# An HBM-to-HBM half shift on one core: two DMA queues of 256-row copies become one queue of 512-row copies with an uneven start

## The chip, the core and the metric

The kernel runs on one core of a Trainium2 chip. It uses no compute engine for the data: everything is done by DMAs from one tensor in HBM to another, carried out by the core's 16 DMA engines. The DMAs are issued by two instruction sequencers, SP (SyncE, `nc.sync`) and ACT (ScalarE, `nc.scalar`); each of them feeds its own queue, which the profile calls q1 (SP) and q10 (ACT), and both queues run on the same 16 DMA engines. The metric is the device time in microseconds (us).

## The reference

```
x: 8192 x 8192, float32
out = np.fft.ifftshift(x)
```

Both sides are even, so this is a shift by half in both directions: `out[r, c] = x[(r + 4096) % 8192, (c + 4096) % 8192]`. The four quadrants of the matrix change places diagonally. No number is changed. A row is 32 KB (32,768 bytes), half a row 16 KB (16,384 bytes); the matrix is 268.44 MB, which is read once and written once, as 16,384 half rows.

## The kernel before

The work is cut into blocks of 256 rows (`ENGINES * per` = 16 x 16). For each of the 32 blocks, two DMAs are issued, one on each queue: one copies the left halves of the 256 output rows (from the right halves of the source rows), the other the right halves (from the left ones). In even blocks SP has the left halves and ACT the right ones, in odd blocks it is the other way round. So each queue gets 32 DMAs of 256 half rows, 4 MB each.

The access pattern of a DMA, `[[C, 16], [16 * C, 16], [1, 4096]]`, has 16 as its outermost size, and this is what spreads it over the 16 DMA engines: engine e gets rows e, e + 16, e + 32 and so on of the block, 16 half rows of 16 KB each, and each half row is one packet. At any time the engines thus work on neighbouring rows, and an engine's next packet of the same queue lies 16 rows (512 KB) further on. An engine that has work in both queues takes packets from the two in turn.

The Tile framework gives the DMAs eight semaphores in rotation, four for each queue here. From the fifth DMA of a queue on, the sequencer waits before the issue until the DMA four earlier on that queue has landed. Hence at most four DMAs of a queue are in flight.

Of the kernel before, what the change touches and what calls it, by code (L numbers as in the profile page):

```python
# [1 line left out]

# [4 lines left out]


ENGINES = 16


@with_exitstack
def kernel(
    ctx: ExitStack,
    tc: tile.TileContext,
    x: bass.AP,
    out: bass.AP,
):
    nc = tc.nc
    R, C = x.shape  # L20
    hr = R // 2
    hc = C // 2
    per = 16
    rows = ENGINES * per

    def copy(queue, row, h, step):

        dims = [[C, ENGINES], [step * C, per], [1, hc]]
        queue.dma_start(
            out=bass.AP(out.tensor, out.offset + row * C + h, dims),  # L30
            in_=bass.AP(x.tensor, x.offset + (row + hr) % R * C + hc - h, dims),
        )


    for n, row in enumerate(range(0, R, rows)):
        left = n % 2 == 0
        copy(nc.sync, row, 0 if left else hc, ENGINES)
        copy(nc.scalar, row, hc if left else 0, ENGINES)


# [1 line left out]
_INS = ['x']  # L42
_OUTS = [((8192, 8192), 'float32')]


def kernel(**inputs):
    import numpy as _np
    import concourse.bacc as _bacc
    import concourse.tile as _tile
    from concourse import mybir as _mybir  # L50
    from concourse.bass_utils import run_bass_kernel_spmd as _run

    nc = _bacc.Bacc("TRN2", target_bir_lowering=False, num_devices=1)  # L53
    arrays, args = {}, []
    for name in _INS:
        a = _np.ascontiguousarray(inputs[name])
        if a.dtype.kind in "iu":
            a = a.astype(_np.int64)
        arrays[f"in_{name}_dram"] = a
        args.append(nc.dram_tensor(f"in_{name}_dram", a.shape, _mybir.dt.from_np(a.dtype), kind="ExternalInput").ap())  # L60
    for i, (shape, dtype) in enumerate(_OUTS):
        dt = _mybir.dt.from_np(_np.dtype(dtype))
        args.append(nc.dram_tensor(f"out_{i}_dram", shape, dt, kind="ExternalOutput").ap())
    with _tile.TileContext(nc) as tc:
        kernel(tc, *args)
    r = _run(nc, [arrays], core_ids=[0])
    got = tuple(r.results[0][f"out_{i}_dram"] for i in range(len(_OUTS)))
    return got[0]
```

## Time and profile before

| What | Value |
|---|---|
| Time of three runs | 813.11, 813.71, 814.12 us; median 813.71 us |
| Span of the profiled execution | 813.2 us |
| Bytes read, bytes written | 268.44 MB each, 660 GB/s together over the span |
| DMA packets | 17,408: 16,384 of 16 KB and 1,024 semaphore writes |
| DMA issues | 32 on SP, 32 on ACT, 4096 KB each, about 101 us from issue to landing |
| Work of compute engines | 0.2 us (four small memsets of GpSimd) |

The profile's span runs from the first to the last instruction; the time lies 0.5 us above it in the median. A row of the DMA part names the queue, its packets, the megabytes and the time that its packets took, as a share of the span of all 16 DMA engines. Packets come in two sizes only, so from such a row the mean time of one 16 KB packet can be worked out: share x stretch x 16, divided by the number of packets. The trace also holds start, duration, size and queue of each packet, without the number of the engine.

### The profile page before, as it was taken

What the parts mean: (1) busy time and instruction counts of PE and PEld (TensorE: products, weight loads), DVE (VectorE), ACT (ScalarE), POOL (GpSimd) and SP (SyncE); (2) the same over time, 40 slices, a digit from 0 to 9 for tenths busy, and PEclk for the clock granted to TensorE, in tenths of its full rate; (3) what the DMA queues carried; (4) which work ended last, traced back from release to release, by engine and by line L of the source; (5) the groups of instructions that cost most, each with busy time, mean ns of one, the idle gap of its engine ahead of it and who ended that gap; (6) DMA issues with size and microseconds to landing.
All of it is one profiled execution on the core that took longest, in us unless ns stands there. A gap on an engine that the chain in (4) does not pass through costs nothing. (4 is left out here: it accounts for less than half of the span.)

```text
span 813.2 us, 109 instructions
## 1 busy us (share of the span) xinstructions
POOL 0.2 (0%) x4
## 2 busy tenths in 40 slices
POOL 0000000000000000000000000000000000000000
DMA  9999999999999999999999999999999999999998
GB/s 303 336 326 331 334 329 323 330 338 333 330 333 330 334 334 330 335 334 330 325 338 330 336 330 334 334 333 331 341 331 330 334 334 330 333 328 336 331 334 276
DMA packets 17408, 268.44 MB, mean 330 GB/s; under 512 B 1024, under 2 KB 1024, under 8 KB 1024
## 3 DMA queue, kind: packets, MB, share of 16 engines
q1 hardware_dynamic: 8704, 134.22, 50.4%
q10 hardware_dynamic: 8704, 134.22, 48.6%
HBM read 268.44 MB, written 268.44 MB: 660 GB/s over the span
## 5 line engine op out<-in xcount | busy, mean ns | idle before, releaser
L53 POOL MEMSET const-bfloat16-1.0<- 128x1 bf16 x1 | 0.1, 102 | 0.0
L53 POOL MEMSET const-uint8-127<- 128x1 uint8 x1 | 0.1, 101 | 0.0
L53 POOL MEMSET const-float32-0.0<- 128x1 f32 x1 | 0.1, 99 | 0.2 <-issue 0.2
L53 POOL MEMSET const-float32-1.0<- 128x1 f32 x1 | 0.1, 98 | 0.0
## 6 DMA issues: line engine op xcount, KB each, us to landing
out_dram<-in_x_dram SPq DMA_DIRECT2D x32, 4096.0 KB, 101.2
out_dram<-in_x_dram ACTq DMA_DIRECT2D x32, 4096.0 KB, 101.1
```

The lines of the kernel that those rows point to most:

```text
L53: nc = _bacc.Bacc("TRN2", target_bir_lowering=False, num_devices=1)
```

## The change

All DMAs go on SP's queue; ACT issues none. The left halves of all 8,192 rows are copied first (from row 0 to the end), and then all right halves. A DMA covers 512 half rows, 32 packets an engine (one of them 464, because the left pass of the first 4,096 rows is 48 rows short of eight whole ones).

The first 48 left half rows go in five DMAs of 14, 12, 10, 8 and 4 rows. Their outermost size is that number and not 16, so they lie on the first 14, 12, 10, 8 and 4 engines with one packet each: engines 0 to 3 get five packets, 4 to 7 four, 8 and 9 three, 10 and 11 two, 12 and 13 one, 14 and 15 none. Then the ordinary DMAs begin at row 48, with the same number of packets for every engine (1,021). Altogether there are 37 DMAs instead of 64, on eight semaphores in rotation, so up to eight are in flight, and the ninth and later ones wait for the one eight earlier.

```diff
-    per = 16
-    rows = ENGINES * per
-    def copy(queue, row, h, step):
-        dims = [[C, ENGINES], [step * C, per], [1, hc]]
+    def copy(queue, row, col, dims):
         queue.dma_start(
-            out=bass.AP(out.tensor, out.offset + row * C + h, dims),
-            in_=bass.AP(x.tensor, x.offset + (row + hr) % R * C + hc - h, dims),
+            out=bass.AP(out.tensor, out.offset + row * C + col, dims),
+            in_=bass.AP(x.tensor, x.offset + (row + hr) % R * C + (col + hc) % C, dims),
         )
-    for n, row in enumerate(range(0, R, rows)):
-        left = n % 2 == 0
-        copy(nc.sync, row, 0 if left else hc, ENGINES)
-        copy(nc.scalar, row, hc if left else 0, ENGINES)
+    unlike = (14, 12, 10, 8, 4)
+    steps = 32
+
+    def walk(queue, row, end, col):
+        while row < end:
+            n = min(steps, (end - row) // ENGINES)
+            copy(queue, row, col, [[C, ENGINES], [ENGINES * C, n], [1, hc]])
+            row += ENGINES * n
+
+    row = 0
+    for n in unlike:
+        copy(nc.sync, row, 0, [[C, n], [1, hc]])
+        row += n
+    walk(nc.sync, row, hr, 0)
+    walk(nc.sync, hr, R, 0)
+    walk(nc.sync, 0, R, hc)
```

## The prediction

> **What bounds the kernel now.** I read the page from the top: the span, the slices, the queues, the issues.
>
> ```profile
> span 813.2 us, 109 instructions
> ...
> DMA  9999999999999999999999999999999999999998
> GB/s 303 336 326 331 334 329 323 330 338 333 330 333 330 334 334 330 335 334 330 325 338 330 336 330 334 334 333 331 341 331 330 334 334 330 333 328 336 331 334 276
> DMA packets 17408, 268.44 MB, mean 330 GB/s; under 512 B 1024, under 2 KB 1024, under 8 KB 1024
> ## 3 DMA queue, kind: packets, MB, share of 16 engines
> q1 hardware_dynamic: 8704, 134.22, 50.4%
> q10 hardware_dynamic: 8704, 134.22, 48.6%
> HBM read 268.44 MB, written 268.44 MB: 660 GB/s over the span
> ...
> out_dram<-in_x_dram SPq DMA_DIRECT2D x32, 4096.0 KB, 101.2
> out_dram<-in_x_dram ACTq DMA_DIRECT2D x32, 4096.0 KB, 101.1
> ```
>
> The DMA engines are busy in every slice, at an even rate. A DMA lands 101 us after its issue, four times the 25 us that 32 packets of an engine take (16 of each queue), so the engines always have work waiting and issue bounds nothing after the start. What counts is the time of one 16 KB packet: each engine has 1,024 of them. For q1 it is 0.504 x 813.2 x 16 / 8,192 = 800 ns, for q10 772 ns, the mean 786. In the packet records a third of them take 608 to 615 ns, and hardly any less: this is what an engine takes when nothing is in its way. The other 170 ns of the mean are contention, and 1,024 x 786 ns = 805 us of the span is packets. The rest is 2.2 us before the first packet and some 6 us of end (the last packets of the engines end between 809.2 and 812.0 us), semaphore writes and gaps.
>
> So the question is what the changed pattern does to these 786 ns: one queue, so that at any time all engines write left halves and read right ones (later the reverse), whereas now half the packets in flight do the one and half the other. Two stretches show one queue alone. First, the start; the DMA rows of the stretch from 3 to 5 us, then from 4.9 to 5.5 us and from 5.5 to 6.3 us:
>
> ```profile
> q1 hardware_dynamic: 48, 0.79, 97.9%
> ...
> q10 hardware_dynamic: 15, 0.25, 104.1%
> ...
> q1 hardware_dynamic: 15, 0.25, 101.7%
> ```
>
> While only q1 was there, a packet took 0.979 x 2 x 16 / 48 = 653 ns. Then q10 joined with 666 ns, and the next round of q1 took 868. Second, the end: from 807.3 us on q10 is alone, and 49 packets took 0.390 x 5.9 x 16 / 49 = 751 ns (the semaphore writes are nothing in it).
>
> ```profile
> q10 hardware_dynamic: 65, 0.80, 39.0%
> ```
>
> The rate by stretches (us, length, POOL, clock, DMA share, GB/s written):
>
> ```profile
> 3.10:5.10 2.00, 0.00 (x0) 1.00 1.04 426
> 5.10:7.00 1.90, 0.00 (x0) 1.00 0.91 310
> 9.00:12.00 3.00, 0.00 (x0) 1.00 0.98 328
> 20.00:40.00 20.00, 0.00 (x0) 1.00 0.98 331
> 400.00:420.00 20.00, 0.00 (x0) 1.00 1.01 337
> ```
>
> The 426 GB/s hold for 2 us; 10 us after the start the rate is already that of the whole run.
>
> **The change, part by part.** *The start.* The issues of SP on the time line (start, length, count; four in 2.77 us, so one in 0.69):
>
> ```profile
> 0.73 2.77 SPq L29 DMA_DIRECT2D out_dram<-in_x_dram  x4
> ```
>
> Five small DMAs in front put the first ordinary one's issue at 0.73 + 5 x 0.69 = 4.2 us, and with the 1.44 us that now lie between the first issue and the first packet (2.17 us) its packets begin at 5.6 us. Engines 0 to 3 are then through with their five: 2.17 + 0.97 (first round) + 4 x 0.65 = 5.75 us. Engines 14 and 15 have nothing until 5.6 us. So the issue pitch equals a packet's time, and all engines enter row 48 within about 0.2 us of each other: the five packets of lead are waited off, not kept. If a DMA of 14 rows issues in, say, two thirds of the time (bound: the records show no small one), the spread is about 1.3 us, less than the 2 to 3 us between the first and the last engine that the semaphore landings of one DMA show now anyway. Cost: engines 14 and 15 have 1,021 packets to do at 5.6 us, where they now have about 1,019.2 left (3.4 us at 653 ns, the first 965); engines 0 to 3 have 1,026 instead of 1,024. Both ways about +1.4 us. Between 0 (small issues that are quick) and 2.6 us (engines 14 and 15 idle 3.4 us, only 1 us of it made up).
>
> *Number of DMAs.* 37 instead of 64: 27 semaphore packets of 9 ns fewer for each engine, -0.25 us. Longer DMAs change nothing else: with eight in flight, 256 packets an engine wait instead of 128. The new waits of SP (the ninth DMA for the first, and so on) have only SP's later DMAs behind them and about 200 us of queued work as cover; the ninth's own is over at about 4 us, and three long DMAs (96 packets, 75 us) are queued by then.
>
> *ACT's issues* go; they cost nothing now (cover: the same queued work).
>
> *One queue, one half at a time.* Three readings of a packet:
> - q1's mean, 800 ns. q1 runs ahead: its DMAs land 4.6 us before q10's of the same block, so it is the first to touch a 32 KB row, and q10 follows in the other half. That the follower is 28 ns cheaper can be a gain from the row just visited. With one pass for each half, every packet is a first visit: 14 ns x 1,024 = +14.7 us.
> - Windows of 0.3 us in the records, sorted by how many of the 16 engines are on q1: 335 GB/s at 8 to 10, 320 to 322 at 0 to 4, 331 at 12 to 16, mean 332. The nearer to one queue, the slower: 0.3% to 3.7%, +2 to +30 us. Single packets say so more sharply: a q1 packet that starts with 2 others on q1 takes 753 ns, with 14 others 872.
> - The stretches alone: 653 ns (-136 us) at the start, 751 (-36 us) at the end. The start is three rounds out of an idle memory and its rate is gone 2 us later; at the end engines are already dropping out, which helps those that remain.
>
> I take the first, which lies inside the second and rests on 16,384 packets instead of 97: +14.7. Sum: +1.4 - 0.25 + 14.7 = +15.8 us on the profiled 813.2, 829.0; with the 0.5 us by which the median is above the span, 829.5. Ends: 751 ns gives 813.7 - 36 + 1 = 779, and 320 GB/s gives 813.7 + 30 + 1 = 845.
>
> The Trainium skill (HBM Reference, Specifications) gives about 716 GB/s for a stack; by it an estimate of the packets' least time is 536.9 MB / 716 = 750 us in place of 805, if both tensors share one stack, and the 653 ns of the start, 804 GB/s both ways, could only be a short-lived loan from buffers. No row of this trace shows where the tensors lie.
>
> **The rivals.**
> 1. *Faster: the two halves disturb each other.* With two queues, reads of one fall among writes of the other in the same halves; alone, they are apart. For it: both stretches alone, and the jump from 653 to 868 ns one round after q10 came. Against it: the sorted windows. Price: the end's 751 ns, 779 us; it decides if a packet in mid-run takes less than 785 ns. The start's 653 ns held for all gives 679 us; I give that little.
> 2. *Faster: the lead is kept*, and engines that stand in other row groups collide less. For it: the records' rate swings with a period of 6.3 us, four packets of each queue (64 rows), between 321 and 340 GB/s, so where the rows lie matters. Levelled at the best mixture, 335 GB/s, this is 1% less: 807 us. Against it: the issue arithmetic above, by which the change does not do what it says.
> 3. *No change.* The same 16 engines carry the same bytes at 786 ns: 813.7 + 1.4 - 0.25 = 814.9 us. The flat slices (323 to 341) speak for a limit that no order moves; the 28 ns between the queues against. The Trainium skill says this too (DMA: Bandwidth & Descriptors, Issuing engines are not separate DMA queues): several issuing engines save only issue time; by that rule alone it would be 814.9 us.
>
> **How the numbers follow.** Slower by first visits and by like traffic: 0.51, its own range 818 to 848, with a few in a hundred beyond. Rival 1: 0.30, between 700 and 805. Rival 2: 0.09, 800 to 811. No change: 0.10, of which the start's cost puts 0.04 above the bound. This kernel's measurement can tell about 0.2% (1.6 us) from no change. So faster 0.39, same 0.06, slower 0.55. The likeliest is 829.5. The range leaves out a tenth at each side: 770 to 848.
>
> **What would show it.** The first visits: the queue row of the changed kernel, one queue at a mean of about 800 ns a packet and slices of 322 to 328 GB/s, in both halves of the run; slices of 345 and more are rival 1, and 332 is rival 3. The start: first long packets of all engines at 5.5 to 6 us. The lead: landings of one DMA spread over 2 to 3 us, as now, and not over 4. Issues: 37 on SP, 8,192 KB in the median, about 200 us to landing. The prediction is wrong above all if the cheaper q10 has another cause than the row just visited, such as an order among queues that one queue doesn't have.

## The result: 0.5% slower

| | kernel before | changed kernel |
|---|---|---|
| Median of six runs | 813.63 us | 818.10 us |
| Ratio of the two, 95% interval | | 1.0051 (1.0034 to 1.0068) |
| The same on a second chip, 23 and 12 runs | 810.57 us | 814.53 us |
| Ratio there | | 1.0040 (1.0019 to 1.0061) |
| Span of the profiled execution | 813.2 us | 816.2 us |

The change costs 4.5 us. I had forecast 15.8, so the direction was right and the size more than three times too large. The page of the changed kernel, slices, queue and issues:

```profile
span 816.2 us, 82 instructions
...
DMA  8999999999999999999999999999999999999998
GB/s 275 331 333 327 338 328 334 332 334 336 340 331 332 331 332 328 329 337 332 333 328 328 333 327 330 327 337 331 333 332 334 334 333 331 326 335 328 333 330 272
DMA packets 16944, 268.44 MB, mean 329 GB/s; under 512 B 560, under 2 KB 560, under 8 KB 560
## 3 DMA queue, kind: packets, MB, share of 16 engines
q1 hardware_dynamic: 16944, 268.44, 98.9%
HBM read 268.44 MB, written 268.44 MB: 658 GB/s over the span
...
out_dram<-in_x_dram SPq DMA_DIRECT2D x31, 8192.0 KB, 106.9
```

One queue now carries everything at 0.989 x 816.2 x 16 / 16,384 = 788 ns a packet: neither the 800 of the old q1 nor the 751 of the lone queue at the old end, but the old mean of both queues, 786. The slices after the first are those of before. The first is lower, 275 against 303 GB/s.

So I split the span in its first 10 us, its last 10 us and what lies between. The stretches of the kernel before, then of the changed one (start and end, length, POOL, clock, DMA share, GB/s written):

```profile
0.00:10.00 10.00, 0.20 (x4) 1.00 0.79 280
803.20:813.18 9.98, 0.00 (x0) 1.00 0.64 215
```

```profile
0.00:10.00 10.00, 0.20 (x4) 1.00 0.61 211
806.20:816.17 9.97, 0.00 (x0) 1.00 0.60 204
```

In the first 10 us the changed kernel moves 2.11 MB instead of 2.80. At the later 332 GB/s the missing 0.69 MB are 2.1 us. In the last 10 us it lacks 0.11 MB, 0.3 us. What is left for the middle is 263.5 MB in 793.2 us before (332.2 GB/s) and 264.3 MB in 796.2 us after (332.0 GB/s): 0.6 us. Of the 3.0 us between the spans, the start has two thirds.

The medians differ by 1.5 us more than these two spans. In every other profiled run of this case the time is 1.7 to 1.8 us above the span, so the profiled execution of the kernel before took about 815 us, some 1.3 us more than its median. Of the 4.5 us between the medians, the start and the end thus have about 2.4; the other 2 us (0.25%) lie somewhere in the run, and these two profiles don't show where.

How the start loses them is on SP's time line (start, length, instructions): the first small DMA, the first long one, and then the eighth and ninth together.

```profile
0.73 0.97 SPq L26 DMA_DIRECT2D out_dram<-in_x_dram  x1
...
4.74 0.64 SPq L26 DMA_DIRECT2D out_dram<-in_x_dram  x1
...
6.08 22.25 SPq L26 DMA_DIRECT2D out_dram<-in_x_dram  x2
```

A DMA of 14 rows doesn't issue faster than one of 256: the five take 0.97, 0.80, 0.74, 0.66 and 0.60 us, and the first long one follows at 4.74 us. In the packet records only 4.4 of 16 engines are busy between 5.5 and 6.0 us, and all of them only from 8.5 us on; before, all were busy from 2.5 us. Weighed by engines, the start stands still 2.0 us longer.

### The profile page after: what moved, and what is told of

It is laid out like the page before. It is cut to its first block, busy times and chain, and to the rows that moved or that the text cites. A ratio compares the mean times of both kernels' runs of the same rounds, so it can differ in the third digit from the quotient of the medians.

```text
span 816.2 us, 82 instructions
## 1 busy us (share of the span) xinstructions
POOL 0.2 (0%) x4
## 6 DMA issues: line engine op xcount, KB each, us to landing
out_dram<-in_x_dram SPq DMA_DIRECT2D x31, 8192.0 KB, 106.9
```

## The experiments

The changed kernel itself was among them:

> The changed kernel again, beside the others on one chip. On a chip where the kernel before takes 822 us, 0.4% to 0.6% above it; if the costs add, one queue without the uneven start (0.28%) and its start and end (about 1.1 us, 0.14%) make 0.42%.

Measured: 1.0040 (1.0019 to 1.0061), as in the table above. In its first 10 us it moved 193 GB/s, where `e5_two_halves` (below), without the uneven start, moved 275 on the same chip. At 332 GB/s the missing 0.82 MB are 2.5 us.

The chips differ: the kernel before takes 811 to 823 us on them. Each ratio is taken on one chip, against runs of the kernel before there.

### Undoing the uneven start

`e1_plain` is the changed kernel with

```diff
-    unlike = (14, 12, 10, 8, 4)
+    unlike = ()
```

> The changed kernel without the uneven start: one queue, 512 rows a DMA, left halves then right ones. If the uneven start alone costs the time (idle engines at the start, a wider end) and one queue is free: 814 to 815 us, mean packet 786 to 788 ns, landings of a DMA spread over 2 to 3 us. If one queue with one half at a time costs the 2 ns a packet that the changed kernel shows, and the start nothing: 816 to 818 us. If the uneven start has hidden what I forecast for one queue, so that engines in step suffer: packets of 800 ns and 825 to 830 us.

Measured: 1.0028 (1.0008 to 1.0048), and 797 ns a packet on a chip where the kernel before takes 822.5 us:

```profile
span 824.4 us, 77 instructions
...
q1 hardware_dynamic: 16896, 268.44, 99.1%
...
0.00:10.00 10.00, 0.20 (x4) 1.00 0.82 280
```

The last line is its first 10 us: without the five small DMAs it moves 280 GB/s there, as the kernel before does, and not 211. So the loss at the start belongs to the uneven start.

> One queue, 512 rows a DMA, left halves then right ones, no uneven start, again. If the single queue costs something of its own: 0.1% or more above two queues with the same order of halves, which run beside it. If the order of halves is all there is: both 0.15% to 0.3% above the kernel before.

The second time, on another chip, it was 1.0019 (0.9999 to 1.0039). So one queue without the uneven start is about 0.2% slower than the kernel before, hardly more than can be told from nothing, and the rival that in-step engines suffer is out in the size expected (825 to 830 us where the kernel before takes 814). Something smaller of the kind isn't excluded: in the two profiles of this kernel the rate from 20 to 200 us is 321 and 326 GB/s, and 329 to 331 later, a rise that the two profiles of the changed kernel don't have (331 to 333 throughout). With the uneven start the ratio is 1.0051 and 1.0040, some 0.2% higher, which fits the 2.0 us of the start; the differences are near their intervals' width, so the first 10 us of the profiles are the stronger evidence for it.

### The first visit to a row

`e3_far` takes away the second visit, on which I had put the forecast:

```diff
-        copy(nc.scalar, row, hc if left else 0, ENGINES)
+        copy(nc.scalar, (row + hr) % R, hc if left else 0, ENGINES)
```

> The kernel before, but ACT copies the half rows of a block 4,096 rows away from SP's, so that no engine's queue comes back to a 32 KB row that the other has just visited. If the second visit to a row is what makes q10 28 ns cheaper than q1 (the step of the prediction): both queues near 800 ns and 825 to 829 us. If the difference belongs to the queues or their order: q1 again near 800, q10 near 772, and 812 to 815 us.

Measured: 1.0004 (0.9985 to 1.0023). The queues:

```profile
span 821.2 us, 109 instructions
...
q1 hardware_dynamic: 8704, 134.22, 49.8%
q10 hardware_dynamic: 8704, 134.22, 49.4%
```

That is 798 and 792 ns. The expected 825 to 829 us were 1.4% to 1.9% above the 814 us of the kernel before, and nothing of this came. That both queues are near 800 ns is no sign of it: the chip is slower, the kernel before takes 822.5 us there, and by this its mean packet would be 786 x 822.5 / 813.7 = 794 ns (an estimate, it has no profile on that chip). The mean of `e3_far` is 795.

Nor does the gap between the queues come from the second visit alone. `e5_two_halves` (below) copies all left halves before the right ones, so no queue comes back to a row that the other has just visited, and still one queue is cheaper:

```profile
span 810.8 us, 109 instructions
...
q1 hardware_dynamic: 8704, 134.22, 50.2%
q10 hardware_dynamic: 8704, 134.22, 49.0%
```

These are 795 and 776 ns, and 797 and 791 in its second profile. The gap differs between two profiles of one program, and with every packet a first visit the measured ratios are 1.0001 to 1.0017. The step is refuted: 800 ns wasn't the price of a first visit. What sets the gap stays open.

### What the total is: fewer engines, and reads alone

If the total is fixed, engines that take less than their part must run undisturbed. `e4_twelve` copies with 12 engines, the kernels below with 13 and 14 (the edit is on the kernel before; `...` stands for lines left out):

```diff
-    for n, row in enumerate(range(0, R, rows)):
...
+    def walk(queue, row, end, col):
+        while row < end:
+            n = min(32, (end - row) // 12)
+            if n:
+                dims = [[C, 12], [12 * C, n], [1, hc]] if n > 1 else [[C, 12], [1, hc]]
+                size = 12 * n
+            else:
+                size = end - row
+                dims = [[C, size], [1, hc]]
...
+            row += size
+
+    walk(nc.sync, 0, hr, 0)
+    walk(nc.sync, hr, R, 0)
+    walk(nc.sync, 0, hr, hc)
+    walk(nc.sync, hr, R, hc)
```

> One queue, left halves then right ones, no uneven start, but only 12 of the 16 DMA engines, 1,364 packets each. If a limit on all traffic together (332 GB/s each way) sets the packet's 786 ns: twelve engines at the undisturbed 611 ns would move 322 GB/s, below the limit, so packets of 611 to 640 ns and 845 to 885 us. If each engine is held up by every other one it meets: 611 + 175 x 11/15 = 739 ns and about 1,015 us.

```profile
span 838.4 us, 93 instructions
...
GB/s 277 323 312 314 321 326 322 326 322 323 324 323 324 323 323 324 323 325 322 324 324 324 324 324 324 324 323 323 325 322 325 322 325 322 325 322 325 323 325 255
...
q1 hardware_dynamic: 16928, 268.44, 74.9%
```

840.2 us for one run, a little under the expected 845 to 885, beside 822.5 of the kernel before on that chip. The packets take 0.749 x 838.4 x 16 / 16,384 = 613 ns, in the records 99% of them at the undisturbed 611. A quarter of the engines is gone, the time is 2% longer, and the contention has vanished.

> As with twelve engines, but 13 engines, 1,260 packets each. Undisturbed they would move 349 GB/s each way, above what 16 engines get. If all traffic together has a fixed limit near 330 GB/s: packets near 640 ns and 815 to 828 us, as 16 engines. If it is the crowding of 16 engines that lowers the limit: packets of 611 to 625 ns and 780 to 800 us, 3% to 5% under the kernel before.

> 14 engines, 1,170 packets each; undisturbed 376 GB/s each way. Fixed limit: packets near 690 ns and 815 to 828 us. Crowding: packets between those of 13 and 16 engines, and 790 to 815 us.

Measured: 1.0236 (1.0203 to 1.0268) and 1.0362 (1.0329 to 1.0395), slower than either expectation. The slices of the 13 engines:

```profile
GB/s 281 330 330 335 331 337 335 333 331 336 331 332 333 330 334 333 335 335 333 331 336 331 331 336 334 334 331 334 319 329 333 332 325 329 331 336 329 323 217 176
...
q1 hardware_dynamic: 17028, 268.44, 79.3%
```

The mean packets, 642 and 681 ns, are as a fixed limit would have them. Through most of the run 13 engines move 332 GB/s, as 16 do, and 14 engines 328 in this stretch from 20 to 780 us:

```profile
20.00:780.00 760.00, 0.00 (x0) 1.00 0.85 328
```

The limit is there: undisturbed they would have moved 349 and 376. The times are longer because the engines don't share it alike. In the landings of the second DMA of 13 engines, 5 engines are done at 43.2 to 43.5 us and 8 at 46.1 to 47.1; the 5 go on at 19.5 us a DMA at first, undisturbed (32 x 611 ns), and the 8 fall ever further behind. At the end these are alone: from 790 to 820 us 8 engines are busy, at 216 GB/s, which is 611 ns a packet. With 14 engines it is 6 and 8. With 16 engines the ends lie within 2 to 3 us. A limit that is dealt out in equal parts to two groups of eight engines would look like this; the records don't number the engines, so that isn't shown.

`e10_loads` replaces the copies by loads of the same half rows into SBUF (the core's own memory), in DMAs of 128 rows on both queues:

```diff
...
+            t = pool.tile([128, hc], mybir.dt.float32, name="rows")
+            queue = nc.sync if h == 0 else nc.scalar
+            queue.dma_start(
+                out=t[:, :],
+                in_=bass.AP(x.tensor, x.offset + row * C + h, [[C, 128], [1, hc]]),
+            )
...
```

> The reads alone: every half row of x goes to SBUF instead of the output, and only the last 128 rows are written to HBM, so the output is left out but for those. If the limit of 16 engines is on reads and writes together (664 GB/s): packets at the undisturbed 611 ns and 630 to 660 us. If it is on each direction (332 GB/s): near 815 us.

```profile
GB/s 373 427 428 431 430 426 426 433 429 427 427 433 429 427 427 429 432 427 426 429 431 429 427 428 429 430 428 427 430 431 428 426 430 430 428 427 430 429 429 334
...
HBM read 268.44 MB, written 4.19 MB: 425 GB/s over the span
```

643.9 us for one run, 425 GB/s: without the writes to HBM all 16 engines run at nearly their undisturbed rate (16 x 16,384 B / 611 ns = 429 GB/s). The Trainium skill (HBM Reference, Specifications) has the same figure, about 425 GB/s for a core that streams alone, bounded by its engines; this run agrees. So neither the engines nor the reads by themselves set the copy's 332 GB/s; it takes the writes to HBM. Whether the writes alone are held to 332 GB/s, or reads and writes together to some 664, isn't shown: no run here writes without reading.

### Whether rows matter at all

`e8_pitch32` and `e8_pitch33` give the engines other rows, on two queues; `pitch` is 32 or 33:

```diff
+    pitch = 32
+
+    def run(queue, row, h, k, count):
+        dims = [[k * C, ENGINES], [C, count], [1, hc]]
...
+            k = min(pitch, (half + hr - row) // ENGINES)
+            for first, count in ((0, 16), (16, k - 16)):
+                left = n % 2 == 0
+                run(nc.sync, row + first, 0 if left else hc, k, count)
+                run(nc.scalar, row + first, hc if left else 0, k, count)
...
```

> The kernel before with other rows for each engine: a block has 512 rows, engine e takes rows 32e to 32e+15 and then 32e+16 to 32e+31, so engines stand 1 MB apart and walk neighbouring rows. If the limit is on bytes, whatever their rows: 0.99 to 1.01 of the kernel before. If it comes from engines in step meeting in the memory (Trainium skill, DMA: Bandwidth & Descriptors, Latency and other measured facts, HBM row pitch at large powers of two): clearly slower, 1.03 to 1.3.

> The same with a pitch of 33 rows, 1 MB and 32 KB, so that engines in step stand in different places modulo 512 KB. Limit on bytes: 0.99 to 1.01. If meetings in the memory count, this is back at the kernel before (0.99 to 1.01) where the pitch of 32 is slower, or below 0.99.

Measured: 1.2248 (1.2162 to 1.2335) and 1.0256 (1.0197 to 1.0314). The totals, at a pitch of 32 rows and of 33:

```profile
HBM read 268.44 MB, written 268.44 MB: 538 GB/s over the span
```

```profile
HBM read 268.44 MB, written 268.44 MB: 636 GB/s over the span
```

So the limit is not on bytes whatever their rows: engines 1 MB apart get 538 GB/s, 32 KB more between them gives back 636, not quite the rate of neighbouring rows that had been expected (660, on a faster chip; the ratios are the fair measure). This agrees in kind with the Trainium skill (DMA: Bandwidth & Descriptors, Latency and other measured facts, HBM row pitch at large powers of two), where a few KiB more of pitch bring back the full rate. The change left the engines on neighbouring rows, and the rate stayed, which fits.

### The order of halves, the queue, the lead

`e5_two_halves` has two queues, but left halves first:

```diff
-    for n, row in enumerate(range(0, R, rows)):
-        left = n % 2 == 0
-        copy(nc.sync, row, 0 if left else hc, ENGINES)
-        copy(nc.scalar, row, hc if left else 0, ENGINES)
+    for h in (0, hc):
+        for n, row in enumerate(range(0, R, rows)):
+            copy(nc.sync if n % 2 == 0 else nc.scalar, row, h, ENGINES)
```

> Two queues as before, blocks of 256 rows in turn on SP and ACT, but all left halves first and then all right ones. If the 0.28% of one queue without the uneven start comes from copying one half at a time: 0.2% to 0.4% above the kernel before. If it comes from the single queue: no difference from the kernel before (under 0.15%).

> Two queues, left halves first and then right ones, no uneven start, again. Order of halves as the cause: 1.0015 to 1.003, as one queue. Single queue as the cause: 0.999 to 1.001.

1.0017 (0.9997 to 1.0037) and 1.0001 (0.9980 to 1.0021): nothing that these runs can tell. The one queue of `e1_again` stood 0.18% above it on the same chip, within what the intervals allow for chance. Whether a single queue costs a little by itself stays open, and with it the 2 us that start and end don't explain.

`e2_skew_two` puts the uneven start alone on the kernel before. `f1_lead10` doubles it: two packets for each engine of each small DMA, and 10 instead of 13 in the DMA behind them. `f2_halves_skew` joins it with left halves first. The edit of `e2_skew_two`, where `part` copies n engines' rows with a given number of packets each:

```diff
...
+    at = 0
+    for n in (14, 12, 10, 8, 4):
+        part(nc.sync, at, 0, n, 1)
+        at += n
+    part(nc.sync, at, 0, ENGINES, 13)
+    copy(nc.scalar, 0, hc, ENGINES)
     for n, row in enumerate(range(0, R, rows)):
+        if n == 0:
+            continue
...
```

> The kernel before with the uneven start alone: SP's first left block goes as DMAs of 14, 12, 10, 8, 4 and 208 rows, all else as it was on two queues. If the uneven start costs what the changed kernel shows at its ends: 814.7 to 816 us, with the landings of a DMA spread over 3 to 4 us. If the start is free because ACT's queue gives the idle engines work: 813 to 814 us. If the uneven start brings something of its own, below 812 us.

> The kernel before with the uneven start alone, a second time on another chip or day. If the 0.18% of the first time is real: ratio 0.996 to 0.9995. If it was chance: 0.999 to 1.002, as a limit on all traffic would have it, plus under 0.1% for the start.

> The kernel before with a doubled uneven start: SP's first left block in DMAs of 28, 24, 20, 16, 8 and 160 half rows, so engines have 0 to 10 packets ahead on SP's queue. If a lead lowers the packet's time: ratio 0.992 to 0.997, and a mean packet at or below that of the single lead; the wider end takes back up to 2 us. If the earlier gain was the start's idle time alone or chance: 0.998 to 1.003.

> Two queues, left halves first and then right ones, with the uneven start: the changed kernel but for its single queue and the size of its DMAs. If the start's gain holds whenever two queues run: 0.997 to 1.000. If it needs the two halves of a row in flight together: 1.0015 to 1.004, as without the start or above.

| | ratio to the kernel before |
|---|---|
| uneven start on two queues | 0.9982 (0.9966 to 0.9998) |
| the same, second time | 0.9962 (0.9931 to 0.9993) |
| doubled uneven start on two queues | 1.0069 (1.0043 to 1.0096) |
| uneven start, two queues, left halves first | 0.9989 (0.9969 to 1.0008) |

The uneven start alone is faster than both kernels, by 0.2% and 0.4% against the kernel before; both intervals end just short of 1. With left halves first (the last row) the ratio can't be told from 1. On two queues the uneven start costs next to nothing: with ACT's first long DMA issued beside the small ones, idle engines have work (272 GB/s in the first 10 us of `e2_skew_two`, 280 in `e1_plain` on that chip). And the lead is kept there: the landings of one of SP's DMAs spread over 7 us, over 3.6 and 3.0 us in the two profiles of the changed kernel, over 2.3 us before. Twice the lead (12 us of spread or more) is slower, outside both of its expectations, so "more lead, faster" is refuted as a rule; what the single lead gains by isn't settled. The queues of the single and of the doubled lead:

```profile
q10 hardware_dynamic: 8704, 134.22, 50.1%
q1 hardware_dynamic: 8752, 134.22, 49.0%
```

```profile
q10 hardware_dynamic: 8704, 134.22, 50.6%
q1 hardware_dynamic: 8752, 134.22, 48.5%
```

Now q10 is the dearer one (804 ns, q1 786), in the faster kernel. The mean is 795 ns, as that of `e3_far` on the same chip, where q1 was the dearer: once more the gap between the queues says nothing on the time.

## Why the prediction was wrong

**The bound.** Right: the packet's 786 ns against the undisturbed 611 is what the time consists of, and issue bounds nothing after the start. What I called contention is a limit on the copy as a whole: twelve engines stay just under it and run undisturbed, thirteen reach it, and the loads show that it takes the writes.

**The steady rows, +14.7 us.** This is the step that failed (14 x 1,024 are 14.3; the 14.7 need 14.4 ns). I took q1's 800 ns as the price of a first visit, and the packet came out at 788; of the 4.5 us between the medians some 2 us at most are left for the steady rows. Under a common limit a faster queue makes the other one slower, and only the mean of both is a price. In `e5_two_halves` every packet is a first visit, the gap is there all the same, and the time is 0.0% to 0.2% longer; in `e2_skew_two` the gap is turned round, and the kernel is faster. That the direction came out right is owed to the start and to a remainder of unknown cause, and not to the step that carried 14.7 of the 15.8 us.

**The sorted windows.** They misled in the same way. A packet that starts among 14 of its own queue takes longer, but the windows with one queue in the majority are brief moments of a run whose mean over 12 us hardly varies, and all engines on one queue all the time gave 332 GB/s, the old mean. Nor did they say clearly what I read: with 12 to 16 engines on q1 they had 331 GB/s, hardly less than the mean. 0.3% to 3.7% was read from them; one queue without the uneven start shows 0.2% to 0.3% over the whole time.

**The start, +1.4 us, bounds 0 to 2.6.** Right in kind and in its bounds, low in size: 2.0 us. I had the issue pitch from the long DMAs (0.69 us) and thought that small ones might be quicker; they took 0.80 us in the mean from issue to issue, and the first packet came 1.71 us after its issue (at 2.44 us) and not 1.44. So the long packets came later, and all engines worked from 8.5 us on, not from 5.5 to 6. The end, for which I had no term, costs 0.3 us.

**The lead.** Half right. I said that it would be waited off. Most engines do enter the long DMAs together (in the second long DMA's landings 13 of 16 lie within 1.5 us), but the last three follow up to 3.7 us behind the first and stay so to the end of the run. I had said 2 to 3 us, not over 4; the median is 3.6, and 3.0 on the second chip.

**Issue to landing, forecast 200 us.** Wrong: 106.9 us. I took eight DMAs in flight from the semaphores, but these don't hold SP back now: the ninth issue itself takes 21.6 us, and the later ones 20 to 28 us, about as long as a DMA of 32 packets an engine runs. When it ends, at 28.3 us, an engine has had time for some 28 of the 128 packets of the first four long DMAs, so about 100 are waiting (an estimate from these times, at 788 ns a packet). That is enough: the engines are busy throughout the middle of the run.

**The rivals.** No change (814.9 us, chance 0.10) was nearest in mechanism: the rate of the bytes stayed. The Trainium skill's rule behind it (DMA: Bandwidth & Descriptors, Issuing engines are not separate DMA queues) holds here to 0.2% or 0.3%. The faster rival, from the 653 and 751 ns of one queue alone, is refuted with the forecast: both stretches were the edges of the run. Rival 2, the kept lead, had its levelled rate of 335 GB/s in view; the changed kernel has 332. On two queues, where the lead is kept, something is gained, but 0.2% to 0.4% and not the 1% that I gave it.

## What to carry to other kernels

When many streams share one limit, the mean time of one stream's packets is no price: ask first whether the total is fixed, by taking engines away until the packets run undisturbed, and then change only what can move the total. Here that was where the engines' rows lie (19% between two pitches), and not the queue, the order of halves and the size of a DMA, which all together moved the time by 0.2% to 0.3%. What then remains is the start and the end: several small DMAs in front of the first large one on a single queue cost their issue times in idle engines, unless another queue has work out by then.

## What was not expected of the hardware

- Twelve of the 16 DMA engines copy HBM to HBM at 320 GB/s each way, 16 at 326 to 331 on the chips of these runs; 13 and 14 end no sooner than 12, because 5 or 6 engines go on undisturbed, 8 are slowed, and the shares of work are equal.
- An issue takes 0.6 to 1.0 us at the start, of 4 rows as of 512, and SP's issue of 32 packets an engine blocks for 20 to 28 us once about 100 packets an engine are queued (the estimate above).
- 32 KB more between the engines' rows, on 1 MB, changes the copy from 538 to 636 GB/s.
